# A bias table moved into the first stage and a first row of x loaded in two halves, in a one-core attention block

## The chip, the cores and the metric

The kernel runs on one core of one Trainium2 chip. The metric is device time in microseconds (us) of one execution; smaller is better. Three executions of the kernel before the change took 791.22, 792.78 and 794.69 us, so the time before is a median of 792.78 us.

The engines are called PE (TensorE, matrix products), DVE (VectorE), ACT (ScalarE), POOL (GpSimd) and SP (SyncE, which here only starts transfers). Each takes its instructions strictly in the order of its own queue, so an instruction that waits holds up everything behind it on its engine. Transfers (DMAs) are started by SP, ACT or POOL and run on 16 shared DMA engines.

## The reference, cut to what matters

One layer of a sliding-window attention block, for 512 tokens of width 2048:

```
hn = rmsnorm(x, norm_g)                               # norm_g: one gain per column of x
q, k, v, gate = split(hn @ w_in)                      # 32 heads on 4 key/value heads
bias   = rel_bias[bucket(distance)]                   # one row of 128 distances per head
scores = q @ k * 64**-0.5 + bias                      # only distances 0..127 are seen
probs  = softmax(scores, with one sink per head)
y      = ((probs @ v) * silu(gate)) @ w_out
x      = x + y
x      = x + (p @ ple_proj) * sigmoid(rmsnorm(x, ple_norm) @ ple_gate)
out    = rmsnorm(x, final_g)
```

All of it is float32. The bias of a score depends only on its head and on the distance between the two tokens.

## The kernel before, in words

**Products.** A float32 operand is split into a high part and a low part (`whi`/`wlo` of the weights, `xh`/`xl` of x), and each product is done as three: high by high (L124), high by low (L125), low by high (L126). ACT makes a high part by a cast, DVE the low part by a subtraction.

**The first stage** (lines 186 to 246) goes over 16 row blocks of x transposed, `k` = 0 to 15, each of 128 rows. For each, SP loads 512 columns of x and one column of `norm_g` behind them (`xr`, L190, from the input `in_xT` of width 513) and 768 columns of weights (`w0`, L195): 256 for keys, 256 for values and 256 for the first two blocks of queries. ACT multiplies x by the gain into `xh` (L199), DVE makes `xl` (L203), ACT and DVE split the weights into `w0s` (L207, L208), and PE adds up queries (`qps`), keys (`ktps`) and values (`vps`) over all 16 blocks. These tiles rotate through three buffers each. For `k` = 0 the query columns of the weights come on ACT's own queue (L137), are split by DVE (L201, L202), and the query products are written in an order of their own (L216): high weights by high x for both query blocks, low weights by high x, high weights by low x. Before them PE runs 34 small products on constants (`WARM`, L145).

In the same stage the rows of x are loaded once more in plain order (`xn`, L236, at `k` = 3 to 6), ACT sums their squares (L237), and DVE makes `rstd1` from that at `k` = 9. POOL writes it to DRAM and reads it back spread over all partitions: `rdram` (L241), then `rb` (L242). Everything that is later taken out of the sums is multiplied by `rb`.

**The bias table** (L317 to L331) stands behind the first stage in the program. POOL loads `rel_bias` (L320) into a quarter of the four large buffers (`misc`), fills a table of 384 columns per head with a large negative number (L321), copies in one value per distance (L324, and 16 copies in L329), and writes the table to DRAM (`tdram`, L331). SP reads it back in skewed form as `bias` (L378, `load_bias`): once before the attention loop for the first group of heads, and then once for each further group.

**The attention stage.** SP's order there is the order in which the code is written. At its start stand four copies of weights inside DRAM (`sum_weights`, L672; POOL adds a second weight block to each by an accumulating transfer, L674), then `load_bias(0)`, then the loads of weights: `wraw` (L101), three buffers, split by ACT (L107) into `whi` and by DVE (L113) into `wlo`, three buffers each. PE runs query and gate projections out of these, each block of 1024 weights giving eight steps of three products, and one step of attention between stretches of them: transposes (L478), probabilities by values (L522, L524, the second with a masked copy `own` made by POOL in L502), scores (L400). The parts after it (out projection, second gate, final norm) aren't touched.

PE and SP follow the order written in the program; in the first stage the order on ACT, DVE and POOL is set by a scheduler.

Of the kernel before, what the change touches and what calls it, by code (L numbers as in the profile page):

```python
# [11 lines left out]
F32 = mybir.dt.float32  # L12
# [7 lines left out]
S = 512  # L20
P = 128
KC = D // P
NB = S // P
HEADS = 32
# [9 lines left out]
BUCKETS = 32  # L34
MAX_DIST = 128
WINDOW = 128
PLE = 256
EPS = 1e-6
MASKED = -3.0e38
TOEP = 384  # L40
WARM = 34
PAD = 32


# [11 lines left out]
def trunk_kernel(ctx: ExitStack, tc: tile.TileContext, a: dict):  # L56
    nc = tc.nc
# [22 lines left out]
    def quarter(name):  # L80
        return whole.tile([P, 4, S], F32, tag="quarter", name=name)
# [92 lines left out]

    kinds, upto = [], {"q": 2, "g": 0}
    for kind in "qq" + "qqqqggg" * (KVH - 1) + "ggggggg":
        kinds.append((kind, upto[kind]))
# [6 lines left out]
    for k in range(KC):  # L186
        both = start_pool.tile([P, 2, 768], F32R, tag="w0s", name=f"w0s{k}")
        wh, wl = both[:, 0], both[:, 1]
        xg = start_pool.tile([P, S + 1], F32, tag="xr", name=f"xr{k}")
        nc.sync.dma_start(xg, a["xT"][k * P : (k + 1) * P, :])  # L190
        xr, g1 = xg[:, :S], xg[:, S:]
        w0 = w0s[0] if k == 0 else start_pool.tile([P, 768], F32, tag="w0", name=f"w0_{k}")
        cuts = [slice(512, 768), slice(0, 512)] if k == 0 else [slice(0, 768)]
        for c in cuts[-1:]:
            nc.sync.dma_start(w0[:, c], a["w_first"][k][:, c])  # L195
# [3 lines left out]
        nc.scalar.mul(h, xr, g1)  # L199
        if k == 0:  # L200
            nc.vector.tensor_copy(wh[:, cuts[0]], w0[:, cuts[0]])  # L201
            nc.vector.tensor_sub(wl[:, cuts[0]], w0[:, cuts[0]], wh[:, cuts[0]].bitcast(F32))  # L202
        nc.vector.scalar_tensor_tensor(  # L203
            out=l, in0=xr, scalar=g1, in1=h.bitcast(F32), op0=ALU.mult, op1=ALU.subtract
        )
        for c in cuts[-1:]:
            nc.scalar.copy(wh[:, c], w0[:, c])  # L207
            nc.vector.tensor_sub(wl[:, c], w0[:, c], wh[:, c].bitcast(F32))  # L208
        xh.append(h)
        xl.append(l)  # L210
        f, e = k == 0, k == KC - 1
        qc = [slice(512 + t * P, 512 + (t + 1) * P) for t in range(2)]
        if f:
            for n, (sw, mx) in enumerate(((wh, h), (wl, h), (wh, l))):
                for t in range(2):
                    nc.tensor.matmul(q_ps[t], sw[:, qc[t]], mx, start=n == 0, stop=False)  # L216
        else:
            for t in range(2):
                mm3(q_ps[t], wh[:, qc[t]], wl[:, qc[t]], h, l, f, e)
# [13 lines left out]
        if 3 <= k < 3 + NB:  # L233
            t = k - 3
            xn = quarter(f"xn{t}").rearrange("p k t -> p (k t)")
            nc.sync.dma_start(xn, a["x"][t * P : (t + 1) * P, :])  # L236
            nc.scalar.activation(xn, xn, AF.Square, accum_out=ssq1[:, t : t + 1])  # L237
        if k == 9:
            run(rsqrt_mean(rstd1, ssq1, D, "r1"))
            rdram = tc.dram_tile([NB, P], F32, name="rdram")  # L240
            nc.gpsimd.dma_start(rdram.rearrange("t p -> p t"), rstd1)  # L241
            nc.gpsimd.dma_start(rb, rdram.rearrange("t p -> (t p)").partition_broadcast(P))  # L242
# [77 lines left out]
    nc.gpsimd.dma_start(relb, a["rel"])  # L320
    nc.gpsimd.memset(tvec, MASKED)  # L321
    exact = BUCKETS // 2
    bk = bucket_of(np.arange(WINDOW))
    nc.gpsimd.tensor_copy(tvec[:, P - 1 : P - 1 + exact], relb[:, :exact])  # L324
    for b in range(exact, BUCKETS):
        d = np.nonzero(bk == b)[0]
        if len(d):
            lo, n = P - 1 + int(d.min()), len(d)
            nc.gpsimd.tensor_copy(tvec[:, lo : lo + n], relb[:, b : b + 1].to_broadcast([HEADS, n]))  # L329
    tdram = tc.dram_tile([HEADS, TOEP], F32, name="tdram")  # L330
    nc.gpsimd.dma_start(tdram, tvec)  # L331

    pre.close()
    banks_s.close()
# [1210 lines left out]
    n = done[3]  # L1545
# [42 lines left out]
def laid_out(i):  # L1588

    f = lambda v: np.ascontiguousarray(v)  # L1590
    w = np.asarray(i["swa_w_in"])[0]
    tiles = lambda v: f(v.reshape(KC, P, -1, P).transpose(2, 1, 0, 3).reshape(-1, P, KC * P))
    quads = lambda v: f(
        np.asarray(v).reshape(8, 2, P, 4, 512).transpose(3, 0, 2, 1, 4).reshape(4, 8, P, 1024)
    )
    qw = HEADS * HD
    kvw = KVH * HD
    x = np.asarray(i["x"])[0]
    cols = lambda v: f(np.asarray(v).reshape(KC, P).T)
# [33 lines left out]
```

## Time and profile before

| | |
|---|---|
| three executions | 791.22, 792.78, 794.69 us |
| the profiled execution, its own time | 791.03 us |
| its span, first to last instruction | 789.3 us |
| PE busy | 778.5 us, 99% |
| DVE, ACT, POOL busy | 623.7, 506.5, 180.4 us |
| moved by transfers | 206.99 MB, 262 GB/s on average |
| granted TensorE clock | 0.997 |

In the rows of the profile "us" are microseconds from the span's start. A row of the timeline gives start, busy time, engine, line, operation and tiles, and in square brackets how long the engine had been idle and what ended that. A row of the waits gives who waited for whom, the total, the number of times and the longest. "SPq" and "POOLq" are the transfer issues of these engines. PE rows are modelled pipelines: products overlap, so the step from one start to the next is the cost of one, not its busy time.

### The profile page before, as it was taken

How to read it: one execution, taken by the hardware profiler on the slowest of the kernel's cores; microseconds unless marked ns; L12 is line 12 of the kernel's file. 1: busy time of each engine (PE TensorE's matmuls, PEld its weight loads, DVE VectorE, ACT ScalarE, POOL GpSimd, SP SyncE). 2: the span in 40 equal slices, each digit the busy share in tenths (PEclk: the TensorE clock that was granted, in tenths of full speed). 3: DMA queues.
4: the chain of work that ended last, by engine and by line, in shares of the span. 5: the costliest groups of instructions: out<-in, count | busy, mean ns of one | idle time of the engine just before them, and what ended most of it. 6: DMA issues, size and time to landing. Idle time of an engine off the chain costs nothing.

```text
span 789.3 us, 11284 instructions
## 1 busy us (share of the span) xinstructions
PE 778.5 (99%) x3726; PEld 650.0 (82%) x3726; DVE 623.7 (79%) x1056; ACT 506.5 (64%) x1024; POOL 180.4 (23%) x394
## 2 busy tenths in 40 slices
PE   9999999999999999999999999999999999999995
PEld 8888788888888888888888888888888888888885
DVE  4446468887977788787886798999798988999686
ACT  5632366667666666565665655767788857967465
POOL 0002423544344414444143300200000021101000
PEclk9999999999999999999999999999999999999998
DMA  8797799999999999989997497998778999967833
GB/s 332 282 251 189 259 280 331 297 290 300 305 312 245 309 268 275 278 212 246 294 245 208 136 352 288 245 367 281 249 272 248 365 238 251 255 227 215 256 117 118
DMA packets 50634, 206.99 MB, mean 262 GB/s; under 512 B 7264, under 2 KB 8416, under 8 KB 44208
## 3 DMA queue, kind: packets, MB, share of 16 engines
q1 hardware_dynamic: 40240, 156.15, 54.7%
q0 software_dynamic: 9904, 49.61, 32.8%
q8 instruction: 29, 0.48, 0.2%
q10 hardware_dynamic: 432, 0.52, 0.2%
q14 instruction: 29, 0.24, 0.1%
HBM read 199.38 MB, written 78.69 MB: 352 GB/s over the span
## 4 chain that ended last, share of the span: by engine, by line
PE 92%; DMA 3%; DVE 2%; ACT 1%; issue 1%; SPq 0%; POOL 0%; ACTq 0%; DVEq 0%; POOLq 0%
PE gps L124 7%; PE gps L125 7%; PE gps L126 7%; PE qps L124 6%; PE qps L125 5%; PE qps L126 5%; PE g L125 5%; PE o L124 5%; PE g L124 5%; PE g L126 5%; PE o L125 5%; PE o L126 5%; DMA wraw<-in_w_q 2%; PE vps L228 2%; PE s L400 2%; PE o L522 2%
## 5 line engine op out<-in xcount | busy, mean ns | idle before, releaser
L124 PE MATMUL gps<-xh,whi 128*128 128x512 f32 x256 | 100.5, 393 | 0.0
L125 PE MATMUL gps<-xl,whi 128*128 128x512 f32 x256 | 100.1, 391 | 0.0
L126 PE MATMUL gps<-xh,wlo 128*128 128x512 f32 x256 | 99.9, 390 | 0.0
L113 DVE TENSOR_TENSOR wlo<-wraw,whi 128x1024 fp32r<-128x1024 f32 x60 | 74.6, 1246 | 30.5 <-ACT whi L107 17.2
L502 POOL TENSOR_SCALAR_AFFINE_SELECT own<-r 64x256 fp32r<-64x256 f32 x96 | 60.1, 626 | 162.2 <-DVE r L491 82.7
L126 PE MATMUL qps<-xh,wlo 128*128 128x512 f32 x224 | 87.5, 391 | 0.5 <-DVE wlo L113 0.5
L124 PE MATMUL qps<-xh,whi 128*128 128x512 f32 x224 | 87.7, 391 | 0.0
L125 PE MATMUL qps<-xl,whi 128*128 128x512 f32 x224 | 87.5, 391 | 0.0
L460 ACT ACTIVATE t<-t,sm 128x129 f32<-128x129 f32 x128 | 50.7, 397 | 51.7 <-DVE sm L451 48.8
L107 ACT CAST whi<-wraw 128x1024 fp32r<-128x1024 f32 x60 | 62.2, 1038 | 20.9 <-DMA wraw<-in_w_q 20.9
L710 DVE TENSOR_TENSOR blo<-braw,bhi 128x1024 fp32r<-128x1024 f32 x43 | 52.7, 1229 | 14.9 <-ACT bhi L709 14.9
L709 ACT CAST bhi<-braw 128x1024 fp32r<-128x1024 f32 x43 | 45.0, 1050 | 28.9 <-DMA braw<-in_ple_gate 9.5
L710 DVE TENSOR_TENSOR blo<-ring,bhi 128x1024 fp32r<-128x1024 f32 x48 | 58.3, 1223 | 4.7 <-ACT bhi L709 4.3
L709 ACT CAST bhi<-ring 128x1024 fp32r<-128x1024 f32 x48 | 50.2, 1049 | 17.9 <-PE o L126 14.1
L124 PE MATMUL g<-bhi,fhg 128*128 128x512 f32 x148 | 58.0, 392 | 0.0
L125 PE MATMUL g<-blo,fhg 128*128 128x512 f32 x148 | 57.8, 391 | 0.0
L126 PE MATMUL g<-bhi,flg 128*128 128x512 f32 x148 | 57.7, 390 | 0.0
L126 PEld LDWEIGHTS gps<-xh,wlo 128*128 128x128 f32 x256 | 48.1, 188 | 10.5
L124 PEld LDWEIGHTS gps<-xh,whi 128*128 128x128 f32 x256 | 48.1, 188 | 9.1
L483 ACT CAST r<-pt 128x256 fp32r<-128x256 f32 x64 | 23.8, 371 | 49.5 <-PE pt L478 49.3
L125 PEld LDWEIGHTS gps<-xl,whi 128*128 128x128 f32 x256 | 48.1, 188 | 8.6
L126 PEld LDWEIGHTS qps<-xh,wlo 128*128 128x128 f32 x224 | 42.1, 188 | 10.0 <-DVE wlo L113 1.0
(303 smaller groups left out, 2034.4 us busy)
## 6 DMA issues: line engine op xcount, KB each, us to landing
w_out<-in_w_out POOLq DMA_DIRECT2D x32, 512.0 KB, 9.2
wraw<-in_w_gate_in SPq DMA_DIRECT2D x32, 512.0 KB, 7.7
ring<-w_out SPq DMA_DIRECT2D x32, 512.0 KB, 4.7
wraw<-in_w_q SPq DMA_DIRECT2D x28, 512.0 KB, 9.3
braw<-in_ple_gate SPq DMA_DIRECT2D x22, 512.0 KB, 5.2
ring<-in_w_out SPq DMA_DIRECT2D x18, 512.0 KB, 5.5
ple_gate<-in_ple_gate SPq DMA_DIRECT2D x16, 512.0 KB, 10.0
ple_gate<-in_ple_gate POOLq DMA_DIRECT2D x16, 512.0 KB, 7.9
```

Source lines behind the costliest of these rows:

```text
L107: nc.scalar.copy(hi, self.raw[i])
L113: nc.vector.tensor_sub(lo, raw, hi.bitcast(F32))
L124: nc.tensor.matmul(ps, sh, mh, start=first, stop=False, skip_group_check=more)
L125: nc.tensor.matmul(ps, sh, ml, start=False, stop=False, skip_group_check=more)
L126: nc.tensor.matmul(ps, sl, mh, start=False, stop=last, skip_group_check=more)
L228: nc.tensor.matmul(v_ps[t], h[:, c], both[:, :, 256:512], start=f, stop=e, skip_group_check=True)
L400: nc.tensor.matmul(s_ps[:, u, : 2 * n], st, key[:, :, first : first + n], start=True, stop=True)
L460: nc.scalar.activation(su, su, AF.Exp, bias=sm[:, u : u + 1], accum_out=sm[:, 2 + u : 3 + u])
L483: nc.scalar.copy(r[:, 0], PT[i])
L502: nc.gpsimd.affine_select(out=cols(own[places[g % 2 ^ low]]), in_=cols(r[here, low].bitcast(F32)), pattern=[[sign * QB, 2], [0, GROUP], [s ...
L709: nc.scalar.copy(hi, raw)
L710: nc.vector.tensor_sub(lo, raw, hi.bitcast(F32))
```

## The change

Four edits, made together:

- The bias table is made by a function that is called in the first stage, at `k` = 8, ahead of the code for `rdram` and `rb`; it no longer stands behind the first stage.
- The column of `norm_g` comes first in `in_xT` and not last, and block 0 of x is loaded in two transfers, the gain with the first 256 columns and then the other 256, both on SP's queue. SP's issues were one row long for this block and are two.
- For `k` = 0, ACT makes `xh` in two halves, and the high by high query products are four of 256 columns, first half for both query blocks and then the second half, where there were two of 512.
- `WARM` is 33.

```
-WARM = 34
+WARM = 33
...
+    xg0 = start_pool.tile([P, S + 1], F32, tag="xr", name="xr0")
+    nc.sync.dma_start(xg0[:, :257], a["xT"][:P, :257])
+    nc.sync.dma_start(xg0[:, 257:], a["xT"][:P, 257:])
...
+    def bias_table():
+
+        misc = quarter("misc")
+        relb, tvec = misc[:HEADS, 1, :BUCKETS], misc[:HEADS, 2, :TOEP]
+        nc.gpsimd.dma_start(relb, a["rel"])
+        nc.gpsimd.memset(tvec, MASKED)
...
+        tdram = tc.dram_tile([HEADS, TOEP], F32, name="tdram")
+        nc.gpsimd.dma_start(tdram, tvec)
+        return tdram
...
-        xg = start_pool.tile([P, S + 1], F32, tag="xr", name=f"xr{k}")
-        nc.sync.dma_start(xg, a["xT"][k * P : (k + 1) * P, :])
-        xr, g1 = xg[:, :S], xg[:, S:]
+        if k == 0:
+            xg = xg0
+        else:
+            xg = start_pool.tile([P, S + 1], F32, tag="xr", name=f"xr{k}")
+            nc.sync.dma_start(xg, a["xT"][k * P : (k + 1) * P, :])
+        xr, g1 = xg[:, 1:], xg[:, :1]
...
-        nc.scalar.mul(h, xr, g1)
+        both_halves = (slice(0, 256), slice(256, 512))
+        for c in both_halves if k == 0 else (slice(0, 512),):
+            nc.scalar.mul(h[:, c], xr[:, c], g1)
...
-            for n, (sw, mx) in enumerate(((wh, h), (wl, h), (wh, l))):
+            for c in both_halves:
                 for t in range(2):
-                    nc.tensor.matmul(q_ps[t], sw[:, qc[t]], mx, start=n == 0, stop=False)
+                    nc.tensor.matmul(q_ps[t][:, c], wh[:, qc[t]], h[:, c], start=c.start == 0, stop=False, skip_group_check=True)
+            for sw, mx in ((wl, h), (wh, l)):
+                for t in range(2):
+                    nc.tensor.matmul(q_ps[t], sw[:, qc[t]], mx, start=False, stop=False, skip_group_check=True)
...
+        if k == 8:
+            tdram = bias_table()
         if k == 9:
             run(rsqrt_mean(rstd1, ssq1, D, "r1"))
...
-    misc = quarter("misc")
-    relb, tvec = misc[:HEADS, 1, :BUCKETS], misc[:HEADS, 2, :TOEP]
-    nc.gpsimd.dma_start(relb, a["rel"])
...
-    tdram = tc.dram_tile([HEADS, TOEP], F32, name="tdram")
-    nc.gpsimd.dma_start(tdram, tvec)
...
-        "xT": f(np.concatenate([x.T, np.asarray(i["norm_g"][0])[:, None]], axis=1)),
+        "xT": f(np.concatenate([np.asarray(i["norm_g"][0])[:, None], x.T], axis=1)),
```

Two side effects follow from where tiles are allocated. The large buffer that `misc` takes is the one that held the first `xn` tile, so its load waits for ACT's sum of squares of that tile. And block 0's x tile is now allocated ahead of its split weights, which changes the layout of the first stage's buffers; the first `bias` tile, which reuses their room, used to lie on split weights that PE reads until the end of the stage, and now lies on x tiles that DVE and ACT have read some time before.

On POOL, around the hand-over from the first stage to the attention stage, there stood before (names are tiles, with running numbers; `ple_gate` and `small` are weight sums in DRAM):

```order
L241 DMA rdram<-rstd_143 128x4x1
L242 DMA rb<-rdram 128x512
L674 DMA ple_gate_0_0_746<-in_ple_gate 64x2048
L674 DMA ple_gate_0_1_747<-in_ple_gate 64x2048
L674 DMA ple_gate_0_2_748<-in_ple_gate 64x2048
L674 DMA ple_gate_0_3_749<-in_ple_gate 64x2048
L320 DMA misc<-in_rel 32x32
L321 MEMSET misc 32x384
L324 COPY misc<-misc 32x16
```

The table began behind `rb` and four adding transfers. On POOL, the end of the table and what follows it, now:

```order
L194 COPY misc<-misc 32x12
L194 COPY misc<-misc 32x14
L194 COPY misc<-misc 32x15
L196 DMA tdram<-misc 32x384
L273 DMA rdram<-rstd_145 128x4x1
L274 DMA rb<-rdram 128x512
L691 DMA ple_gate_0_0_749<-in_ple_gate 64x2048
```

The whole table, from its load to its store, has moved ahead of `rdram` and `rb`; nothing else on POOL has changed its place.

On SP, at the very start of the program, there stood before:

```order
L190 DMA xr_146<-in_xT 128x513
L195 DMA w_0_95<-in_w_first 128x512
L190 DMA xr_178<-in_xT 128x513
L195 DMA w_1_180<-in_w_first 128x768
L190 DMA xr_209<-in_xT 128x513
```

And on SP now:

```order
L140 DMA xr_97<-in_xT 128x257
L141 DMA xr_97<-in_xT 128x256
L220 DMA w_0_95<-in_w_first 128x512
L215 DMA xr_181<-in_xT 128x513
L220 DMA w_1_183<-in_w_first 128x768
```

One issue has been added, and every later load of SP stands one issue further back.

On PE, from the last product on constants to the first key product, there stood before:

```order
L145 MATMUL warm_ps<-const-bfloat16-1.0 128x128
L216 MATMUL qps_135<-xh_149,w0s_145 128x512
L216 MATMUL qps_136<-xh_149,w0s_145 128x512
L216 MATMUL qps_135<-xh_149,w0s_145 128x512
L216 MATMUL qps_136<-xh_149,w0s_145 128x512
L216 MATMUL qps_135<-xl_150,w0s_145 128x512
L216 MATMUL qps_136<-xl_150,w0s_145 128x512
L124 MATMUL ktps_137<-xh_149,w0s_145 128x512
```

And on PE now (high and low weights lie in one tile, `w0s`, so the rows don't tell them apart: the first two products before, and the four half ones now, take the high weights, the two full ones after them the low weights):

```order
L149 MATMUL warm_ps<-const-bfloat16-1.0 128x128
L243 MATMUL qps_137<-xh_149,w0s_147 128x256
L243 MATMUL qps_138<-xh_149,w0s_147 128x256
L243 MATMUL qps_137<-xh_149,w0s_147 128x256
L243 MATMUL qps_138<-xh_149,w0s_147 128x256
L246 MATMUL qps_137<-xh_149,w0s_147 128x512
L246 MATMUL qps_138<-xh_149,w0s_147 128x512
L246 MATMUL qps_137<-xl_150,w0s_147 128x512
```

Two products of full width have become four of half width; the rest of PE's order is the same to the end of the program.

More of the change, by code (lines that the diff above doesn't have):

```diff
@@ L173, in rsqrt_mean @@
         nc.vector.tensor_mul(out, y, t)
+    def bias_table():
[3 more added lines that the diff above has]
+        nc.gpsimd.memset(tvec, MASKED)
+        exact = BUCKETS // 2
+        bk = bucket_of(np.arange(WINDOW))
+        nc.gpsimd.tensor_copy(tvec[:, P - 1 : P - 1 + exact], relb[:, :exact])
+        for b in range(exact, BUCKETS):
+            d = np.nonzero(bk == b)[0]
+            if len(d):
+                lo, n = P - 1 + int(d.min()), len(d)
+                nc.gpsimd.tensor_copy(tvec[:, lo : lo + n], relb[:, b : b + 1].to_broadcast([HEADS, n]))
+        tdram = tc.dram_tile([HEADS, TOEP], F32, name="tdram")
+        nc.gpsimd.dma_start(tdram, tvec)
+        return tdram
     kinds, upto = [], {"q": 2, "g": 0}
@@ L213, in trunk_kernel @@
         if f:
-            for n, (sw, mx) in enumerate(((wh, h), (wl, h), (wh, l))):
+            for c in both_halves:
                 for t in range(2):
-                    nc.tensor.matmul(q_ps[t], sw[:, qc[t]], mx, start=n == 0, stop=False)
+                    nc.tensor.matmul(q_ps[t][:, c], wh[:, qc[t]], h[:, c], start=c.start == 0, stop=False, skip_group_check=True)
+            for sw, mx in ((wl, h), (wh, l)):
+                for t in range(2):
+                    nc.tensor.matmul(q_ps[t], sw[:, qc[t]], mx, start=False, stop=False, skip_group_check=True)
         else:
             for t in range(2):
-                mm3(q_ps[t], wh[:, qc[t]], wl[:, qc[t]], h, l, f, e)
+                mm3(q_ps[t], wh[:, qc[t]], wl[:, qc[t]], h, l, f, e, True)
         for t in range(2):
@@ L315, in trunk_kernel @@
     split(V[0], values[0])
-    misc = quarter("misc")
-    relb, tvec = misc[:HEADS, 1, :BUCKETS], misc[:HEADS, 2, :TOEP]
[L320 to L329, printed above, removed]
-    tdram = tc.dram_tile([HEADS, TOEP], F32, name="tdram")
-    nc.gpsimd.dma_start(tdram, tvec)
     pre.close()
```

## The prediction

> **What bounds the kernel now.** I read the chain of waits first, then the waits of PE, then those of SP's queue, then the timeline where they point. The shares of the chain that ended last, from the page:
>
> ```profile
> PE 92%; DMA 3%; DVE 2%; ACT 1%; issue 1%; SPq 0%; POOL 0%; ACTq 0%; DVEq 0%; POOLq 0%
> ```
>
> PE sets the time; the change can win only where PE stands or crawls. These are all the waits of PE but the one for the program's start, and under them the longest wait of SP for one thing:
>
> ```profile
> PE qps L126 <- DVE wlo L113: 0.5, 1, 0.5
> PE o L524 <- POOL own L502: 0.3, 1, 0.3
> PE qps L216 <- ACT xh L199: 0.2, 1, 0.2
> SPq L378 <- DMA tdram<-misc: 27.2, 1, 27.2
> ```
>
> PE loses 1.0 us in three places. None of them names the bias table, but SP stood 27.2 us for it, with the weight loads queued behind.
>
> **Term 1, the table.** Before, in order of time: the copies that SP issued last, POOL's table, the weight loads with which SP then went on, and the first of these (the fourth weight block) through ACT and DVE to PE.
>
> ```profile
> 51.55 3.46 SPq L672 DMA_DIRECT2D ple_gate<-in_ple_gate  x4
> 65.78 0.80 POOL L320 DMA_DIRECT2D misc<-in_rel  x1
> 80.39 0.54 POOL L331 DMA_DIRECT2D tdram<-misc  x1 [0.30 <-POOL misc L329]
> 83.15 0.87 SPq L101 DMA_DIRECT2D wraw<-in_w_q  x2
> 87.01 1.05 ACT L107 CAST whi<-wraw 128x1024 fp32r<-128x1024 f32 x1 [13.07 <-DMA wraw<-in_w_q]
> 88.09 1.23 DVE L113 TENSOR_TENSOR wlo<-wraw,whi 128x1024 fp32r<-128x1024 f32 x1 [11.91 <-PE qps L125]
> 71.81 0.40 PE L124 MATMUL qps<-xh,whi 128*128 128x512 f32 x1
> 88.15 0.45 PE L124 MATMUL qps<-xh,whi 128*128 128x512 f32 x1
> 89.37 0.51 PE L126 MATMUL qps<-xh,wlo 128*128 128x512 f32 x1 [0.53 <-DVE wlo L113]
> 89.95 0.40 PE L125 MATMUL qps<-xl,whi 128*128 128x512 f32 x1
> ```
>
> From 71.81 to 88.15 PE makes three weight blocks of 24 products each: 16.34 / 72 = 0.227 us a step. The four steps from 88.15 to 89.95 took 1.80 and should take 0.91: 0.89 us lost, because the fourth block was loaded at 83.15.
>
> After: the table's load on POOL waits for ACT's first sum of squares and for nothing else. That sum, `rdram` and `rb` on POOL, the use of `rb`, the time that transfers into `rdram` and `rb` took from issue to landing (`rb` the shortest, `rdram` the longest), and the first `wlo`:
>
> ```profile
> 15.53 0.18 ACT L237 ACTIVATION_READ_ACCUMULATOR xn<-xn 128x1 f32 x1
> 37.68 0.95 POOL L241 DMA_DIRECT2D rdram<-rstd  x1 [36.30 <-DVE rstd L173]
> 50.94 0.58 POOL L242 DMA_DIRECT2D rb<-rdram  x1 [12.31 <-DMA rdram<-rstd]
> 68.56 1.44 DVE L257 TENSOR_TENSOR rawq<-qps,rb 128x256 f32<-128x256 f32 x4 [4.91 <-PE qps L126]
> DMA to landing us min/median/max: 6.4/9.7/13.0
> 58.42 1.23 DVE L113 TENSOR_TENSOR wlo<-wraw,whi 128x1024 fp32r<-128x1024 f32 x1 [2.65 <-ACT whi L107]
> ```
>
> From the load's issue to the store's issue the table took 80.39 - 65.78 = 14.6 us before, and to SP's next load 17.4. Started at 15.7 it is stored at about 30 and has been read on by 33, while POOL did nothing until 37.68. So `rdram` isn't delayed, and SP issues the bias at about 55.1, right behind the four copies (51.55 + 3.46). The next wait is then the weight buffers': the fourth load needs the first `wlo` (58.42 + 1.23 = 59.65), so it goes out at 59.7 and not at 83.15, 23 us sooner. Its split now waits for a `whi` buffer, free when PE leaves the first block at 71.81 + 24 x 0.227 = 77.3; with 1.05 + 1.23 us for the two splits it is there at 79.6, and PE wants it at 88.6. The whole 0.89 us goes (ends: 0, if another wait takes the place, and 0.89). Queued behind it on SP are two weight loads and two copies into DRAM; they too need only the second and third `wlo`.
>
> POOL and DVE slow each other: a `wlo` took 1.66 us while POOL made `diffs`, against 1.23 alone. The small copies of the table (16 in 2.08 us, and a few more) now run beside DVE's splits of the first stage, so up to about 2.3 x 0.35 = 0.8 us of DVE delay. PE has no wait for DVE there, with x and weights three buffers deep, so I take 0.
>
> ```profile
> 93.12 1.66 DVE L113 TENSOR_TENSOR wlo<-wraw,whi 128x1024 fp32r<-128x1024 f32 x1 [1.27 <-ACT whi L107]
> 78.02 2.08 POOL L329 COPY misc<-misc 32x3 f32<-32x3 f32 x16
> 93.77 1.61 POOL L354 TENSOR_TENSOR diffs<-values 64x256 f32<-64x256 f32 x1
> ```
>
> **Term 2, the echo at 131 us.** The chain before it, and PE at the first two steps with `own` and at an undisturbed one:
>
> ```profile
> 104.87 12.18 DMA wraw<-in_w_q
> 131.21 0.56 PE L522 MATMUL o<-r,V 128*128 128x256 f32 x2
> 132.26 0.43 PE L400 MATMUL s<-k,q 128*128 128x288 f32 x2
> 136.74 0.48 PE L522 MATMUL o<-r,V 128*128 128x256 f32 x2
> 137.44 0.43 PE L400 MATMUL s<-k,q 128*128 128x288 f32 x2
> 141.94 0.48 PE L522 MATMUL o<-r,V 128*128 128x256 f32 x2
> 142.38 0.43 PE L400 MATMUL s<-k,q 128*128 128x288 f32 x2
> 75.00:80.00 5.00, 5.00 (x24) 4.13 (x23) 1.18 (x4) 0.00 (x0) 2.11 (x17) 1.00 0.05 10
> ```
>
> From `o` to the next scores is 0.44 undisturbed, and was 1.05 and 0.70: 0.61 + 0.26 = 0.87 us lost, behind a weight block that took 12.18 us to land. That load shared the DMA engines with everything that SP had sent out in one burst from 83 on; at 75 to 80 they were 5% busy at 10 GB/s (last row). With the burst spread from 55 on, the load lands sooner and ACT and DVE aren't late at 131. But the splits keep their places in ACT's and DVE's queues, so how much returns is open between 0 and 0.87. I take 0.5, a little over half, since the load is the head of that chain.
>
> **Term 3, the start.** The first product waits for `xh`, and the split of its weights ends shortly before:
>
> ```profile
> 0.85 3.79 PE L145 MATMUL warm_ps<-const-bfloat16-1.0 128*128 128x128 bf16 x34 [0.85 <-PEq L1623]
> 1.26 0.41 SPq L195 DMA_DIRECT2D w<-in_w_first  x1
> 4.10 0.72 ACT L199 ACTIVATE xh<-xr 128x512 fp32r<-128x512 f32 x1 [1.36 <-DMA xr<-in_xT]
> 4.26 0.29 DVE L201 CAST w0s<-w 128x256 fp32r<-128x256 f32 x1 [3.33 <-DMA w<-in_w_first]
> 4.87 1.68 PE L216 MATMUL qps<-xh,w0s 128*128 128x512 f32 x4 [0.24 <-ACT xh L199]
> 6.39 0.62 PE L216 MATMUL qps<-xl,w0s 128*128 128x512 f32 x2
> 8.77 0.96 DVE L208 TENSOR_TENSOR w0s<-w,w0s 128x768 fp32r<-128x768 f32 x1 [0.98 <-ACT w0s L207]
> 10.08 0.39 PE L126 MATMUL qps<-xh,w0s 128*128 128x512 f32 x1
> ```
>
> With half of x, `xh` can be ready by about 4.1 + 0.36 even if the half lands no sooner; the weights' cast ends at 4.55, so PE starts at about 4.6: at most 0.27 us gained. Four half products cost what two full ones did: 34 products of 128 columns in 3.79 us are 0.11 each, so 256 columns are 0.22 and 512 are 0.44 at that rate. Against it: all later loads of SP are issued 0.41 later, the time of one issue. The tight place is block 1's low weights, ready at 9.73 and used at 10.08: 0.35 us of cover. If these came 0.41 late and PE 0.27 early, 10.14 - 9.81 = 0.33 would be lost there, leaving -0.06. The ends are -0.1 and +0.27. I take +0.15, nearer the upper one: x landed at 4.1 though issued before 1.26, so loads stand in line behind each other, and one issued 0.41 later need not land later. One product on constants less costs nothing: it ran while PE would wait.
>
> The first four products step by (6.39 - 4.87) / 4 = 0.38, later ones by 0.23: PE speeds up at about 6 us, 5 us after its first product. The Trainium skill ("TensorE: Matmul & The Clock Gate", Part 1) says that the clock runs at half until a free-running window of about 3.4 us was busy, whatever is issued in it; the trace agrees with half speed (0.11 for 128 columns). By that rule 0.27 us won ahead of the change of speed is worth half, 0.14 us, and the sum would stay within 0.02 of mine.
>
> **Sum.** 0.89 + 0.5 + 0.15 = 1.54 us: a span of 787.8 and a profiled execution of 789.5 against 791.03. That one lies 1.75 below the median of the three runs, so on the median I forecast 792.78 - 1.54 = 791.2, 0.2% less. About 0.5% (4 us) is what a measurement of this kernel can tell from no change.
>
> **Rivals.**
> - *The stall stays* (the change doesn't do what it says): SP's next wait, for `wlo`, holds the loads as the table did. For it: the weight buffers are three deep, and each later load needs another `wlo`. Against: the first of these was ready at 59.65. Gain 0 to 0.2: 792.7.
> - *Slower: the table makes `rb` late.* `rdram` now stands behind the table on POOL. `rb` lands at 50.94 + 6.4 = 57.3 and is first used at 68.56, 11.2 us later; with the 4.7 us between the table's end at 33 and 37.68, it decides once the table takes 16 us longer than its 17.4, and from there each us costs one on PE. For it: `rdram` and `rb` took 13.0 and 6.4 us to land, so transfers on POOL's queue can stand long. Against: none here took twice that. A table that takes 40 us would give about 792.78 - 1.5 + 7 = 798.
> - *The speed-up at 6 us comes later.* Half speed through the rest of block 0 (14 products' worth from 6.39 to about 9.6) would cost 14 x (0.44 - 0.23) = 2.9 us: 794.2. For it: PE's idle gap moves and one product on constants is gone; against: the gap of 0.23 us gets shorter. The Trainium skill's rule of the free-running window, named above, allows this in any run, before and after alike.
> - *More than a burst is smoothed*: the transfers moved into the idle stretch relieve the later stages too. Against: PE waits nowhere after 132. At most 792.78 - 2.0 = 790.8.
>
> **How the numbers follow.** Forecast 0.72, the stall stays 0.10, the later speed-up 0.08, late `rb` 0.04, more smoothed 0.06. The range takes the ends of the terms (0 to 2.0 us of gain) and the spread of the three runs about their median (-1.6 and +1.9), without the outermost of both together: 788.8 to 793.6. Over 0.5% faster needs 788.8, beyond every case without luck in the runs: 0.07. Slower by over 0.5% is late `rb` and a part of the later speed-up: 0.05. The rest, 0.88, is no change.
>
> **What would show it.** Right: no wait of SP for `tdram`; bias issued near 55 and the fourth weight load near 60; the table done on POOL before 33; no wait of PE for `wlo` near 88; the DMA engines busy at 75 to 80; first product near 4.6. Wrong: a wait of PE for `w0s` near 10, `rdram` later than 37.7, a new wait of PE between 60 and 140, or `own` still 0.5 us late at 131.

## The result, and the profile after

The changed kernel takes 791.20 us (median of 14 runs, 790.25 to 792.43), the kernel before, run beside it, 793.43 (14 runs, 790.96 to 797.79). The ratio is 0.9967 with an interval of 0.9954 to 0.9979: 0.3% less, a small gain that is larger than its uncertainty. The forecast was 791.2 us. The profiled execution of the changed kernel took 791.25 us with a span of 789.5; that of before took 791.03 with 789.3. So the two traces to be compared show no gain at all, and the medians show 2.2 us, more than the 1.54 that was forecast: the kernel before was 0.65 us slower here than in the three executions on which the forecast stands. All of this has to be explained.

These are all the waits of PE in the changed kernel; those for `wlo`, `own` and `xh` are gone, the one for `blo` is at 739 us, far behind what was changed. In the waits of SP there is none for `tdram` any more.

```profile
PE warm_ps L149 <- PEq L1640: 0.8, 1, 0.8
PE g L125 <- DVE blo L727: 0.3, 1, 0.3
```

**The table and what stood behind it.** From the timeline of the changed kernel, engine by engine: the table on POOL with `rdram` and `rb`, SP's issues, the fourth weight block on DVE, PE where it uses it, and the DMA engines at 75 to 80 us (share and GB/s are the last two numbers).

```profile
16.84 0.70 POOL L185 DMA_DIRECT2D misc<-in_rel  x1 [15.46 <-ACT xn L267]
22.49 3.37 POOL L194 COPY misc<-misc 32x3 f32<-32x3 f32 x16
26.16 0.53 POOL L196 DMA_DIRECT2D tdram<-misc  x1 [0.31 <-POOL misc L194]
38.34 0.79 POOL L273 DMA_DIRECT2D rdram<-rstd  x1 [11.65 <-DVE rstd L177]
49.95 0.55 POOL L274 DMA_DIRECT2D rb<-rdram  x1 [10.82 <-DMA rdram<-rstd]
57.82 0.71 SPq L395 DMA_DIRECT2D bias<-tdram  x1
61.79 2.33 SPq L101 DMA_DIRECT2D wraw<-in_w_q  x2
79.74 1.24 DVE L113 TENSOR_TENSOR wlo<-wraw,whi 128x1024 fp32r<-128x1024 f32 x1 [2.22 <-ACT whi L107]
89.51 0.39 PE L124 MATMUL qps<-xh,whi 128*128 128x512 f32 x1
89.97 0.39 PE L126 MATMUL qps<-xh,wlo 128*128 128x512 f32 x1
75.00:80.00 5.00, 5.00 (x24) 4.13 (x23) 2.78 (x8) 1.33 (x2) 2.56 (x6) 1.00 1.01 272
```

The table is stored at 26.2, `rdram` still waits for `rstd` and not for the table, SP issues the bias at 57.8 and the fourth weight load at 61.8. The fourth block is split at 81.0 and used at 89.5: 8.5 us of cover where there was a wait. The DMA engines, 5% busy at 75 to 80 us before, are full.

**The echo.** The weight block whose load had taken 12.18 us, on ACT, and PE at the two steps that were disturbed at 131 and 137:

```profile
115.77 1.05 ACT L107 CAST whi<-wraw 128x1024 fp32r<-128x1024 f32 x1
131.66 0.48 PE L539 MATMUL o<-r,V 128*128 128x256 f32 x2
132.10 0.43 PE L417 MATMUL s<-k,q 128*128 128x288 f32 x2
136.63 0.48 PE L539 MATMUL o<-r,V 128*128 128x256 f32 x2
137.07 0.43 PE L417 MATMUL s<-k,q 128*128 128x288 f32 x2
```

ACT no longer waits for that load, and both steps take the undisturbed 0.44.

**The start.** PE, ACT and DVE of the changed kernel, then the DMA engines at 4 to 5 us:

```profile
4.28 1.31 PE L243 MATMUL qps<-xh,w0s 128*128 128x256 f32 x4
5.76 0.62 ACT L234 CAST w0s<-w 128x512 fp32r<-128x512 f32 x1 [1.25 <-DMA w<-in_w_first]
5.96 0.64 PE L246 MATMUL qps<-xl,w0s 128*128 128x512 f32 x2
6.41 0.69 DVE L235 TENSOR_TENSOR w0s<-w,w0s 128x512 fp32r<-128x512 f32 x1 [1.12 <-ACT w0s L234]
7.16 0.50 PE L126 MATMUL ktps<-xh,w0s 128*128 128x512 f32 x1
...
9.21 0.96 DVE L235 TENSOR_TENSOR w0s<-w,w0s 128x768 fp32r<-128x768 f32 x1 [0.26 <-ACT w0s L234]
9.60 0.39 PE L124 MATMUL qps<-xh,w0s 128*128 128x512 f32 x1
10.22 0.51 PE L126 MATMUL qps<-xh,w0s 128*128 128x512 f32 x1
4.00:5.00 1.00, 1.00 (x8) 0.97 (x7) 0.93 (x3) 0.51 (x2) 0.00 (x0) 1.00 0.34 109
```

and before, the same cast on ACT and the same stretch:

```profile
4.98 0.62 ACT L207 CAST w0s<-w 128x512 fp32r<-128x512 f32 x1 [0.15 <-DMA w<-in_w_first]
4.00:5.00 1.00, 0.76 (x7) 0.49 (x5) 0.70 (x3) 0.75 (x2) 0.00 (x0) 1.00 1.02 295
```

PE starts 0.59 us sooner (4.28 for 4.87), but the 512 columns of block 0's weights come 0.78 later, and PE waits for their high and then for their low part (split by 6.38 and 7.10). Block 1 begins at 9.60, against 9.61 before, and then meets its low weights late: they are ready at 10.17, not 9.73. These gaps are too short to stand in the list of waits; they show as steps of 0.33 to 0.39 from one product to the next where 0.23 is usual (7.16 follows 6.77, and 10.22 follows 9.83). All of the head start is gone, and a little more.

From there the first stage itself runs slower. A block of it is 20 products; the first key product of block 1 and that of block 15 are 14 blocks apart. First the changed kernel, then the kernel before:

```profile
11.26 0.39 PE L124 MATMUL ktps<-xh,w0s 128*128 128x512 f32 x1
70.34 0.40 PE L124 MATMUL ktps<-xh,w0s 128*128 128x512 f32 x1
```

```profile
10.99 0.39 PE L124 MATMUL ktps<-xh,w0s 128*128 128x512 f32 x1
69.05 0.39 PE L124 MATMUL ktps<-xh,w0s 128*128 128x512 f32 x1
```

That is 59.08 / 14 = 4.220 us a block against 58.06 / 14 = 4.147, with no wait anywhere: 1.02 us over these blocks, and the forecast had nothing of the kind. The account of the two traces, by the time at which PE reaches a place:

| PE at | before | after | difference |
|---|---|---|---|
| first product | 4.87 | 4.28 | -0.59 |
| first product of block 1 | 9.61 | 9.60 | -0.01 |
| first key product of block 1 | 10.99 | 11.26 | +0.27 |
| first projection product | 71.81 | 73.15 | +1.34 |
| first gate product (`gps`) | 145.41 | 145.03 | -0.38 |
| first product of the second gate | 605.99 | 605.62 | -0.37 |
| last product | 780.05 | 780.31 | +0.26 |

Start and first stage lose 1.34, the stretch behind the table gives 1.72 back, and 0.63 is lost behind 690 us at weight loads that land late. That last loss comes and goes without regard to the change: of the kernels below, all of which do the same work there in the same order, some show it and some don't.

### The profile page after: what moved, and what is told of

Its sections match the earlier page's. It is cut to its first block, busy times and chain, and to the rows that moved or that the text cites. A ratio compares the mean times of both kernels' runs of the same rounds, so it can differ in the third digit from the quotient of the medians.

```text
span 789.5 us, 11292 instructions
## 1 busy us (share of the span) xinstructions
PE 779.4 (99%) x3727; PEld 649.8 (82%) x3727; DVE 622.1 (79%) x1056; ACT 506.2 (64%) x1025; POOL 180.8 (23%) x394
## 4 chain that ended last, share of the span: by engine, by line
PE 91%; DVE 4%; DMA 2%; issue 2%; ACT 1%; ACTq 0%; DVEq 0%
PE gps L124 7%; PE gps L125 7%; PE qps L126 7%; PE gps L126 7%; PE qps L124 7%; PE qps L125 7%; PE o L125 5%; PE o L126 5%; PE o L124 5%; PE g L125 3%; PE g L124 3%; PE g L126 3%; PE s L417 2%; PE o L539 2%; PE vps L258 2%; PE pt L495 2%
```

## The experiments

### The table alone, and the start alone

The kernel before, with only the table moved (the code of `bias_table` as in the change):

```
+        if k == 8:
+            tdram = bias_table()
...
-    misc = quarter("misc")
-    relb, tvec = misc[:HEADS, 1, :BUCKETS], misc[:HEADS, 2, :TOEP]
...
-    nc.gpsimd.dma_start(tdram, tvec)
```

> The kernel before with only the bias table moved to block 8 of the first stage. If the table is the cause of the gain: no wait of SP for tdram, no wait of PE for wlo near 88 us and none for own near 131 us, so 0.89 + 0.87 = 1.8 us shorter than the profiled run of before, and against the median of before 2 us or more, because a late weight load can no longer stop PE. If the gain came from the start instead: within 0.5 us of before.

Measured: 789.74 us (12 runs, 788.85 to 792.23) against 792.71 (29 runs), ratio 0.9961 [0.9942, 0.9981]. It is faster than the kernel before. Its median is also 1.5 us under the changed kernel's, but the two weren't run side by side, and the intervals of their ratios overlap; the profiles say the same, with the first projection product at 71.66 here and at 73.15 in the changed kernel. Its waits of PE, but for the program's start:

```profile
PE g L125 <- DVE blo L715: 0.3, 1, 0.3
PE qps L234 <- ACT xh L217: 0.3, 1, 0.3
```

Blocks of the first stage take 4.147 us, though POOL copies beside DVE there as in the changed kernel: the slower step isn't the table's. One row was not expected: the bias is issued no sooner than 71.85.

```profile
71.85 0.72 SPq L383 DMA_DIRECT2D bias<-tdram  x1
```

With the buffers where they were, the bias has its room on split weights that PE reads until the end of the stage, and SP waits for PE. That is still early enough.

The changed kernel with the table back in its old place, behind the first stage (the edit above, reversed):

> The changed kernel with the bias table back at its old place; the two half loads, the half products, the gain in front and 33 products on constants stay, and so does the new buffer layout. If the start gives nothing: first product near 4.3 us, block 1 of the first stage 0.2 to 0.3 us later than before, each later block 0.07 us longer, PE 1.3 us behind at the end of the stage, and the stall for the fourth weight block unchanged or shorter by that lag: 0 to 1.3 us slower than before. If the start is what gains: 1 us or more faster than before.

Measured: 793.32 us (12 runs, 791.34 to 801.11) against 792.71, ratio 1.0014 [0.9989, 1.0040]: not to be told from the kernel before. The blocks take 4.22 us, the first projection product comes at 73.77, ACT waits 2.69 us for the load of the weight block at 119, and the steps behind it are disturbed. No stall at 88 here: PE arrives 2 us later than before, which covers it. So the start with its buffers brings no gain, and the whole gain is the table's. That the start costs doesn't follow from this time; it is seen in the profiles, in PE's later arrival.

### The kernel before, once more

> The kernel before, unchanged, for a second profile of it. If the profiled run of before was a lucky one: PE waits for wlo or own longer than the 0.8 us seen there, by 1 to 4 us, in the stretch from 88 to 140 us. If its runs differ for another reason: the same waits, and a longer time elsewhere (the first products, or the weight loads after 700 us).

Its profiled execution took 792.74 us. The waits of PE, and the weight block on ACT near 117:

```profile
PE qps L124 <- ACT whi L107: 0.5, 1, 0.5
PE qps L126 <- DVE wlo L113: 0.5, 1, 0.5
...
PE o L524 <- POOL own L502: 0.4, 2, 0.3
PE o L522 <- DVE r L491: 0.4, 1, 0.4
```

```profile
118.34 1.05 ACT L107 CAST whi<-wraw 128x1024 fp32r<-128x1024 f32 x1 [2.12 <-DMA wraw<-in_w_q]
```

The same places, at twice the price. The profile that the prediction was made from was a mild one. The profiles can be put in a row by how long ACT sat idle for that one load. (Four more with the table early, not listed, lose nothing either: their ways are 71.86 to 71.88.) "Way" is the time from the first projection product to the first gate product; where nothing is late it is 71.86, and what is above that is lost behind the table. (The other kernels in this table are described below.)

| table | kernel | ACT waits for the load | way | lost | of it ahead of 119 us (the stall) | behind 119 us (the echo) |
|---|---|---|---|---|---|---|
| early | changed kernel | 0 | 71.88 | 0.0 | 0.0 | 0.0 |
| early | table alone | 0.21 | 71.86 | 0.0 | 0.0 | 0.0 |
| late, bias behind the loads | only SP's order | 1.04 | 71.86 | 0.0 | 0.0 | 0.0 |
| late | split weights 384 bytes further | 1.53 | 72.96 | 1.1 | 0.1 | 1.0 |
| late | before, first profile | 1.59 | 73.60 | 1.7 | 0.9 | 0.8 |
| late | before, once more | 2.12 | 75.51 | 3.7 | 1.7 | 2.0 |
| late | split weights 192 bytes further | 2.27 | 74.15 | 2.3 | 0.8 | 1.5 |
| late | start alone | 2.69 | 73.78 | 1.9 | 0.0 | 1.9 |
| late | gain first | 2.74 | 74.15 | 2.3 | 0.3 | 2.0 |
| late | split weights 96 bytes further | 3.18 | 74.40 | 2.5 | 0.4 | 2.1 |

By and large the echo grows with the wait for the load (last column): a wait of 1.04 us still costs nothing, one of 1.5 us or more costs 0.8 to 2.1. On average the echo is the larger part: in the seven profiles in which the loads stood behind the late table it costs 1.6 us, the stall 0.6. What makes the load later in one execution than in another isn't shown.

### Is it the place of the buffers?

The change allocates block 0's x tile ahead of its split weights, and so moves the three buffers of the split weights from byte 193408 of a partition to 199648. Three kernels on that. First the changed kernel with wider x tiles, so that they lie at 199936, a multiple of 128 as 193408 is:

```
-    xg0 = start_pool.tile([P, S + 1], F32, tag="xr", name="xr0")
+    xg0 = start_pool.tile([P, XW], F32, tag="xr", name="xr0")      # XW = 544
```

> The changed kernel with x's tile 544 columns wide in place of 513, so that the split weights behind it begin on a multiple of 128 bytes again (they begin 32 bytes past a multiple of 64 in the changed kernel). Nothing else is changed. If their place sets the step of the products: blocks of the first stage take 4.15 us and not 4.22, so about 1.07 us faster than the changed kernel. If the longer step has another cause (the x rows read one column further right, the time of day): no difference.

Measured: 790.71 us (12 runs, 790.45 to 791.72), ratio 0.9971 [0.9953, 0.9988]; 4.192 us a block. A part of the longer step comes back, not all, and by this run alone the cause was open. So the other way round, the kernel before with its split weights 96 bytes further on, 32 past a multiple of 64:

```
-    w0s = {0: start_pool.tile([P, 768], F32, tag="w0", name="w0_0")}
+    w0s = {0: start_pool.tile([P, 776], F32, tag="w0", name="w0_0")[:, :768]}
```

> The kernel before, with one thing changed: the tiles of the unsplit weights are 8 columns wider, so the split weights of the first stage lie 96 bytes further on, at 32 bytes past a multiple of 64 as in the changed kernel and not at a multiple of 128. Theory A (the place of the split weights sets the step of PE in the first stage): the blocks of the first stage take 4.22 us each, not 4.147, and the first projection product starts about 1 us later than 71.8, near 72.9. Theory B (the place is nothing; the slower step comes from x read one column further right, or from the later loads): 4.147 us and 71.8.

```profile
11.16 0.39 PE L124 MATMUL ktps<-xh,w0s 128*128 128x512 f32 x1
70.22 0.40 PE L124 MATMUL ktps<-xh,w0s 128*128 128x512 f32 x1
```

59.06 / 14 = 4.219 us: the whole slow-down, from a change that only moves buffers (793.47 us in its one run). The x tiles and two of the three tiles of unsplit weights move along with the split weights here; the table of places below tells them apart. And the changed kernel with every buffer back in its old place:

```
+    both0 = start_pool.tile([P, 2, 768], F32R, tag="w0s", name="w0s0")
     xg0 = start_pool.tile([P, S + 1], F32, tag="xr", name="xr0")
...
-        both = start_pool.tile([P, 2, 768], F32R, tag="w0s", name=f"w0s{k}")
+        both = both0 if k == 0 else start_pool.tile([P, 2, 768], F32R, tag="w0s", name=f"w0s{k}")
```

> The changed kernel, with block 0's tile for split weights taken ahead of its tile for x, so that every buffer of the first stage lies where it lay before the change. Theory A (the places of the buffers set the step): blocks of 4.147 us, first projection product near 72.0 (the start's own small loss of about 0.3 us stays), and a time of about 790.1, 1 us under the changed kernel, 0.3 us over the table alone (789.74). Theory B (x read one column further right): blocks stay at 4.22, and the time at 791.2. By both the bias waits for PE's last product of the first stage and is issued near 72 and not 58, since its room lies on split weights again; the fourth weight load then goes out near 73, 15 us ahead of its use, and PE does not wait for it.

```profile
11.53 0.39 PE L124 MATMUL ktps<-xh,w0s 128*128 128x512 f32 x1
69.61 0.39 PE L124 MATMUL ktps<-xh,w0s 128*128 128x512 f32 x1
```

58.08 / 14 = 4.149 us, and 790.48 us (10 runs, 789.78 to 791.17), ratio 0.9960 [0.9940, 0.9980]. The places of the buffers are the cause. What stays is the start itself: 72.37 at the first projection product, where five profiles with the start of before and the same places had 71.35 to 71.81 (mean 71.64). Ahead of nearly all of the blocks, at the first key product of block 1, the four kernels with the changed start on SP's queue stand at 11.26 to 11.89 (mean 11.50), nine profiles with the start of before at 10.53 to 11.19 (mean 10.91): the start costs about 0.6 us, a mean of few profiles that differ by as much among themselves. The bias waits for PE again (7.0 us), and PE waits for nothing at 88: the early bias of the changed kernel bought nothing.

Does x read one column further right play a part? The kernel before with `norm_g` as the first column, and x still loaded whole:

```
-        xr, g1 = xg[:, :S], xg[:, S:]
+        xr, g1 = xg[:, 1:], xg[:, :1]
...
-        "xT": f(np.concatenate([x.T, np.asarray(i["norm_g"][0])[:, None]], axis=1)),
+        "xT": f(np.concatenate([np.asarray(i["norm_g"][0])[:, None], x.T], axis=1)),
```

> The kernel before, with norm_g as the first column of x and nothing else: x is loaded whole, and read from the second column on. Theory A (places alone): blocks of 4.147 us and the first projection product near 71.8. Theory B (x read one column further right is slower for ACT and DVE and so for PE): blocks of about 4.17 to 4.22, and the casts of x on ACT longer than 0.72 us.

4.147 us a block, the first projection product at 71.59, and 791.92 us in one run. It plays no part in the step.

Which places are good? Two more of the kernel before, with the tile of the unsplit weights 784 and 800 columns wide (the edit of the 96 bytes, with these widths):

> The kernel before, with the unsplit weights' tiles 16 columns wider, so that the split weights of the first stage begin 192 bytes further on, at 193600: a multiple of 64 and not of 128. Theory A (a multiple of 64 is enough for the quick step): blocks of 4.147 us in the first stage and the first projection product at 71.6 to 71.9. Theory B (it takes 128): blocks between 4.15 and 4.22, the first projection product up to 1 us later.

> The kernel before, with the unsplit weights' tiles 32 columns wider, so that the split weights begin 384 bytes further on, at 193792: a multiple of 256, as 199936 was in the aligned version of the changed kernel, whose blocks took 4.192 us. Theory A (that version's rest of 0.045 us a block comes from the place itself, a multiple of 256 being worse than 128 beside one): blocks of about 4.19 us. Theory B (the place is fine, and the rest came from something else in that version, the x tiles now lying ahead of the split weights or wider): 4.147 us.

```profile
10.63 0.39 PE L124 MATMUL ktps<-xh,w0s 128*128 128x512 f32 x1
68.50 0.39 PE L124 MATMUL ktps<-xh,w0s 128*128 128x512 f32 x1
```

These rows are of the first of the two: 57.87 / 14 = 4.134 us, quicker than before. The second takes 58.70 / 14 = 4.193 (11.11 to 69.81), as the wider x tiles did. One run each, 792.02 and 791.56 us. All places together (no profile shows the addresses; their differences follow from the widths of the tiles):

| split weights begin at | remainder by 256 | kernel | us a block |
|---|---|---|---|
| 193600 | 64 | before, 192 further | 4.134 |
| 193408 | 128 | before; table alone; old places | 4.147 |
| 199936 | 0 | changed, wider x | 4.192 |
| 193792 | 0 | before, 384 further | 4.193 |
| 199648 | 224 | changed kernel | 4.220 |
| 193504 | 224 | before, 96 further | 4.219 |

Equal remainders give equal steps, in kernels that differ in everything else that was changed. The other buffers don't fit: in the changed kernel and in the one with wider x the x tiles begin at the same byte, where the split weights lay before, and the steps are 4.220 and 4.192; and the unsplit weights of the changed kernel lie where they lay before the change. That it is the remainder by 256 and by no other number isn't shown by six places; nor is whether it is PE's reading or the writing of ACT and DVE beside it.

### Where the head start went

The changed kernel in the old places, and the second half of block 0's x issued on ACT's queue, so that SP has one issue fewer:

```
-    nc.sync.dma_start(xg0[:, 257:], a["xT"][:P, 257:])
+    nc.scalar.dma_start(xg0[:, 257:], a["xT"][:P, 257:])
```

> As the run with the old places, and the second half of block 0's x is issued on ACT's queue, right behind the weights' query columns, so that SP has as many issues as before the change. Theory A (the loads of the start come late because SP issues each 0.4 us later): first product near 4.3 us, the 512 columns of block 0's weights split near 5.0 as before the change and not at 5.8, no wait of PE between 6 and 11 us, first projection product near 71.2 (0.6 us ahead of 71.8), time about 789.2. Theory B (the two half loads themselves hold up what stands behind them in the DMA engines): the split stays near 5.8, PE waits near 6.4 and 10.2 us as in the changed kernel, first projection near 72.0 and a time of about 790.1.

```profile
4.29 0.78 PE L244 MATMUL qps<-xh,w0s 128*128 128x256 f32 x2
5.47 0.50 PE L244 MATMUL qps<-xh,w0s 128*128 128x256 f32 x2 [0.41 <-ACT xh L227]
9.61 0.40 PE L124 MATMUL qps<-xh,w0s 128*128 128x512 f32 x1
```

```profile
4.91 0.51 ACT L227 ACTIVATE xh<-xr 128x256 fp32r<-128x256 f32 x1 [0.74 <-DMA xr<-in_xT]
5.33 0.61 ACT L235 CAST w0s<-w 128x512 fp32r<-128x512 f32 x1
```

Measured: 789.67 us (9 runs, 789.02 to 790.70), ratio 0.9950 [0.9929, 0.9971]. Neither theory came true whole. The weights are cast at 5.33, not 5.0 and not 5.8, and the waits at 6 to 11 us are gone. So the two half loads alone, wherever they are issued, don't cause those waits. Whether it was SP's later issues or the two halves in one queue isn't told apart, since the edit takes away both; nor is when the weights landed, since ACT, busy until then with the late half of x, doesn't wait for them. But now the second half of x is late (ACT waits for it until 4.91), PE stands in the middle of its first four products, and block 1 begins at 9.61, where it began before the change. The first half product 0.6 us sooner is worth nothing in either form, since what follows isn't there sooner. Against the table alone (789.74, measured at another time) no gain of the halves is seen.

### Only SP's order

The kernel before, with the first bias issued behind the fourth to sixth weight loads; the table stays in its place in the code:

```
-    load_bias(0)
...
+        if n == 2:
+            load_bias(0)
```

> The kernel before, with one thing changed: the first load of the bias is issued by SP behind the fourth to sixth weight loads and not ahead of them; the table itself stays where it was on POOL, from 65.8 to 80.4 us. Theory A (what the change gains is the order on SP's queue alone: nothing should stand behind the wait for the table): the fourth weight load goes out near 60, the DMA engines are busy at 75 to 80 us, PE waits for no weights at 88, and the cast of the weight block at 117 on ACT, which waited 1.6, 2.1, 3.2 and 2.7 us for its load in four profiles of kernels with the table late, waits under 0.5 us; the steps of PE at 122 and 132 are undisturbed. Time about 789.9, like the table alone in its new place (789.74). Theory B (the stall at 88 goes with the queue, but the loss at 122 to 138 comes from POOL, which is behind with its adding transfers as long as the table stands at 65.8): 0.9 to 2 us of the loss remain at 122 to 138, time 790.8 to 792.

Measured: 791.09 us (10 runs, 789.13 to 794.28), ratio 0.9989 [0.9967, 1.0012]. In the profiled execution, the quickest of the ten, the way is 71.86 with nothing lost. But the wide spread stays, and the profile shows why:

```profile
92.81 0.72 SPq L378 DMA_DIRECT2D bias<-tdram  x1
90.00:95.00 5.00, 5.00 (x24) 4.14 (x23) 1.33 (x4) 0.75 (x2) 4.40 (x8) 1.00 0.11 33
```

The table didn't stay from 65.8 to 80.4. POOL now issues an adding transfer of the earlier weight copies ahead of the table's load, at 77.13, and the table is stored at 90.93. SP still waits 12.3 us for it, and the DMA engines are 11% busy at 90 to 95 instead of 5% at 75 to 80. The idle stretch has moved, not gone. ACT still waits 1.04 us for the load near 117, where under 0.5 was expected, and it costs nothing in this execution. In this one execution SP's order is enough against the stall at 88 and the echo; whether it is in all of them is left open, since a hole remains, and the ten runs together can't be told from the kernel before.

### The two together

The table alone, with the split weights at 193600, the quickest place found (784 columns, as above):

> The kernel before with the table alone moved into the first stage, as in the first run, and the split weights of the first stage beginning 192 bytes further on, at 193600. Theory A (the step of PE in the first stage follows the place's remainder by 256 bytes: 0 gave 4.192 us a block, 64 gave 4.134, 128 gave 4.147, 224 gave 4.22): blocks of 4.134 us, first projection product near 71.4, no wait of PE for weights near 88, none for own or r between 115 and 140, and a time of about 789.5, 0.2 us under the table alone. Theory B (4.134 in that one run was chance): blocks of 4.147 and a time of 789.7. By both it beats the kernel before (ratio near 0.996) and is 1.5 us under the changed kernel.

Measured: 789.28 us (12 runs, 788.81 to 789.88) against 792.66 (17 runs), ratio 0.9949 [0.9928, 0.9969]: the lowest median of all, and with a narrow spread. Blocks take 4.133 us (57.86 / 14, from 11.19 to 69.05), as with that place before, and the way is 71.86. The first projection product is at 71.82 and not at the expected 71.4, since PE ran its first products slowly for longer (last section). The 0.46 us to the table alone is within what their runs spread.

## Why the prediction was right, and where it was not

- **The table, term 1.** Right in each step: no wait of SP, the table done before 33 (stored at 26.2), bias near 55 (57.8), fourth weight load near 60 (61.8), its split 8.5 us before its use, the stall gone. The 0.89 us of the first profile is within what the stall costs with the table late, 0.0 to 1.7.
- **POOL beside DVE, taken as 0.** Right: beside DVE the 16 copies took 3.37 us instead of 2.08, and with the table alone the blocks kept their 4.147 us.
- **The echo, term 2.** The mechanism was right, the size was not. The prediction took 0.5 of 0.87. All 0.87 came back, and what comes back in other executions is more: the echo was 1.6 us on average in the seven profiles with the table late and the bias ahead of the loads. The step that failed is the argument that the splits keep their places in the queues, so that some of the loss would stay. None stayed once the load came in time. The upper end of 0.87 was also no bound: it was read from one execution, one of the mildest.
- **The start, term 3.** Wrong in sign: a gain of 0.15 was forecast, with a loss of 0.1 as the lower end, and it is a loss of about 0.6 (11.50 against 10.91 at the first key product of block 1). The first product came even sooner than forecast, 4.28 for 4.6. The step that failed is "one issued 0.41 later need not land later": block 0's weights, issued 0.46 later, were cast 0.78 later. The listed sign of it, a wait of PE for `w0s` near 10, is there, short as it is: the product at 10.22 comes 0.39 after the one before it, and not 0.23.
- **The place of the buffers.** Not in the sum. The part on the change says that the layout moves, and the prediction gives that no price. It cost 1.02 us, more than any one term of the sum.
- **The sum.** The table was the right cause, and that the forecast time was met to the tenth is luck. A gain of 1.54 was forecast on a median of 792.78. By the experiments the table gives 3.0 (792.71 less 789.74), and the start and the places take about 1.5 of it back (791.20 less 789.74, and as much between the first projection products, 73.15 against 71.66); that leaves 1.5 by these medians, which are of different times, and 2.2 side by side (793.43 less 791.20). So a table priced too low was cancelled by a start of the wrong sign and by the places, which had no price; and the 0.7 by which the gain side by side exceeds the forecast is how much slower the kernel before ran beside it. The two traces alone (-0.38 at 145 us, and +0.2 at the end) show no gain: the profile of before was 1.75 us under its median, and that kernel's runs spread. With the table late, runs reach 800 or 801; in the six kernels with the table early no run was over 792.5.
- **The range.** Its lower end doesn't follow from its own words: a gain of 2.0 and runs 1.6 under their median give 789.2 even with the outermost of both together, and 788.8 was written. Nothing that was measured hangs on this.
- **The rivals.** The stall didn't stay, `rb` came at 49.95 as before, and PE reached full speed no later: the changed kernel's full-width products step by 0.24 from 5.96 on, those of before by 0.23 from 6.39 on. That more than the burst is smoothed isn't seen: what is gained up to 145 us doesn't grow behind it (-0.38 and -0.37). The one that came true, a start that costs, wasn't among them.

## What to carry to other kernels

When a queue waits 27 us for one small thing, the first stall behind it can be the smaller part of the price: look at how long the DMA engines stand idle, and at which later load that backlog reaches, and read it from more than one execution. A first instruction that starts sooner is worth nothing unless the loads behind it also come sooner; follow the second and the third. And an edit that only changes the order of allocations changes addresses: compare the step of an undisturbed loop before and after, since nothing in the waits shows it.

## What was not expected of the hardware

- The step of the products in the first stage depends on the byte at which the split weights begin: 4.134 us to 4.220 a block, 2%, with the same instructions and no waits. Outside that stage, on other buffers, it makes no difference: from the first gate product to the first of the second gate all fourteen profiles take 460.58 to 460.62 us.
- A weight load of 512 columns that SP issued 0.46 us later, with two half loads of x ahead of it instead of a whole one, was cast 0.78 later, with ACT waiting for it, and the DMA engines stood at a share of 0.34 at 4 to 5 us, against 1.02 before. Why isn't known; with one half on the other queue the share at 4 to 5 us was 1.41, and the half itself came late.
- PE's rise to full speed came at different times behind the same instructions. These two kernels have the same start; first the kernel with the split weights 192 bytes further, then the one with the table moved besides:

```profile
4.75 1.19 PE L216 MATMUL qps<-xh,w0s 128*128 128x512 f32 x4
5.78 0.62 PE L216 MATMUL qps<-xl,w0s 128*128 128x512 f32 x2
```

```profile
4.71 2.01 PE L234 MATMUL qps<-xh,w0s 128*128 128x512 f32 x4
6.56 0.63 PE L234 MATMUL qps<-xl,w0s 128*128 128x512 f32 x2
```

Four products took 1.03 us in one (0.26 each) and 1.85 in the other (0.46 each), with no wait listed in either. So two executions of one start differed by 0.8 us here, more than the halves of x could win. The Trainium skill ("TensorE: Matmul & The Clock Gate", Part 1) says that the window which decides on the rise is free-running, so that the same kernel shows different numbers of slow products; the two traces agree with that.
